# Token operands of an FFN's down projection: split slice by slice in the next unit, in program order with the weights' splits

## The chip, the cores and the metric

The kernel runs on one core of a Trainium2 chip. The metric is the time of one execution on the device in microseconds. The kernel before was timed in three runs: median 2538.07 us (2537.52 to 2538.74). Traces come from one execution each, taken with the hardware profiler. The names of the engines are those of the profile: PE is TensorE, PEld its weight loads, ACT ScalarE, DVE VectorE, POOL GpSimd, and SP (SPq) the engine whose queue issues nearly all transfers.

## The reference

One layer of a streaming encoder over 576 tokens (512 of a new stream and 64 of a running one, the 16 meta tokens apart), in float32:

```python
o_d = rmsnorm(o_d, lp['diff_subln_g']) * (1.0 - lam_init)
mix = jnp.concatenate([o_d.reshape(B, L, D_DIFF), o_m.reshape(B, L, D_MLA)], axis=-1)
x = x + mix @ lp['w_out']
h = rmsnorm(x, lp['norm_ffn_g'])
x = x + (jax.nn.silu(h @ lp['ffn_w_gate']) * (h @ lp['ffn_w_up'])) @ lp['ffn_w_down']
```

Ahead of it stand an input projection and two groups of attention heads, which the change leaves as they are; behind it one more rmsnorm. The model is 2048 wide (16 rows of 128), the hidden layer 5632 (44 rows of 128). The change is in the last line.

## The kernel before

**Products.** A float32 operand is split into a high part in fp32r, which ScalarE writes (an ACTIVATE copy: `wh` of a weight, `bh` of a token operand), and a low part, which VectorE writes (source minus high part: `wl`, `bl`). A product of two such operands is three matmuls: high by high and token-low by weight-high at line 1126, token-high by weight-low at line 1130. Nearly every instruction of the other engines is issued by a recording wrapper, so that its line is 125; the tiles' names tell them apart.

**Gate and up.** The 5632 hidden columns are worked in 22 units `u` of 256. A unit has two turns, gate (g) and up (u). A turn is one call of `winograd`: a 2 x 2 block product by seven products p instead of eight, in the order p = 1, 2, 4, 5, 6, 3, 7 (`ORDER`, `WIDE`). The tokens stand as two halves of 288 columns. For each p, `lhs(p)` makes the weight operand and splits it (`split_weights`): p = 1, 2, 4 from the loaded weights `raw` (two loads of 1 MB a turn), p = 5, 6, 3, 7 from sums `ws` of them, made by GpSimd and VectorE. Then come 16 matmuls with `wh` and 8 with `wl`, and `take(p, banks)` brings the finished accumulator `m` to the tile `c`: by a ScalarE copy for p = 1, 4, 5, 6, by VectorE additions for p = 2, 3, 7. There are two buffers each of `wh` and `wl`. Behind the gate turn `gated` scales c by the tokens' norm `rb2` (VectorE), takes the silu (ScalarE, c to c) and scales again (GpSimd).

**Down operands.** Behind the up turn GpSimd multiplies the two results and forms four differences of their quarters. The product goes to DRAM as `actspill`, the differences as `sumspill`. The down stage loads each quarter or difference again (144 KB), and `builder` splits it there into `bh` and `bl`, for the block of units that comes next.

**Down.** The 22 units go in blocks of 4, 4, 4, 4, 4, 2. A block runs over eight steps d of 256 output columns; in the first five blocks a step is seven products of 12 matmuls (`down_rows`, in the order `CHAIN`), added to the accumulators `y`, which start from `x2spill`. The last block is plain (`plain_rows`, line 205), with the final norm and the output tiles `ot` behind it (`finish`, transposes at line 1394). The operands of the first block are fetched and split during the up turn of unit 21; after it the pools of the gate and up stage are closed and others opened ("the switch").

**What sets the order.** The framework's scheduler orders each engine's instructions by their dependences and a model of their times, except where an instruction is marked:

```python
    def __getattr__(self, name):
        issue = getattr(self.engine, name)

        def call(*args, **kwargs):
            ins = issue(*args, **kwargs)
            return self.tc.keep_in_program_order(ins) if self.ordered else ins
```

A marked instruction stays behind the one that was written just before it on its engine. All matmuls are marked, and, in the down stage, the splits of token operands (`pin`). The weights' splits and the copies of accumulators are not. All engines execute their own list in its order.

Of the kernel before, what the change touches and what calls it, by code (L numbers as in the profile page):

```python
# [2 lines left out]

# [16 lines left out]
P = 128  # L20
# [111 lines left out]
def encoder_step(  # L132
# [196 lines left out]
    sumspill = dp.tile([FC // 2, P, 4, QH], F32, name="sumspill")  # L329
    mspill = dp.tile([KC, P, TQ], F32, name="mspill")  # L330
# [673 lines left out]
    rb2 = rw.tile([P, TQ], F32, name="rb2")  # L1004
    sq2 = rw.tile([P, TQ], F32, name="sq2")
# [13 lines left out]

    def operand(m, p, src):  # L1020
        hi = bc.tile([P, QH], F32R, name=f"bh{p}_{m}")
        lo = bc.tile([P, QH], F32R, name=f"bl{p}_{m}")
        pin(S.activation(hi, src, AF.Copy))
        pin(V.tensor_tensor(lo, src, f32(hi), op=ALU.subtract))
        operands[m, p] = (hi, lo)
# [41 lines left out]

    def winograd(wpool, spool, raws, slots, take, banks=None, engine=V, step=lambda: None, stag=("ws", 3),
                 chain=()):
# [29 lines left out]
        vs = [r.rearrange("p (m t) (f c) -> p t f m c", t=2, f=2) for r in raws]  # L1099
        n = sum(v.shape[3] for v in vs)  # L1100
        a11, a12, a21, a22 = ([v[:, t, f] for v in vs] for f in range(2) for t in range(2))
        sums = {}

        def lhs(p):
            if p in (1, 2, 4):
                return split_weights(n, {1: a11, 2: a12, 4: a22}[p])
            if p == 5:
                s = sums[1] = subtotal(n, G, ALU.add, a21, a22)
            elif p == 6:
                s = sums[2] = subtotal(n, engine, ALU.subtract, [sums[1]], a11)  # L1110
            elif p == 3:
                s = subtotal(n, V, ALU.subtract, a12, [sums[2]])
            else:
                s = subtotal(n, G, ALU.subtract, a11, a21)
            return split_weights(n, [s])

        shared = {}
        for p, name in chain or [(p, p) for p in ORDER]:
            new = name not in shared
            if first:  # L1120
                shared[name] = banks[p] = shared[name] if not new else pmt()[:, 0:QH]
            wh, wl = lhs(p)
            for k in range(n):
                hi, lo = operands[slots[k], p]
                for x in (hi, lo):
                    PE.matmul(banks[p], wh[:, k, :], x, start=first and new and k == 0 and x is hi, stop=False,  # L1126
                              skip_group_check=not new)
            for k in range(n):
                hi, lo = operands[slots[k], p]
                PE.matmul(banks[p], wl[:, k, :], hi, start=False, stop=last and k == n - 1,  # L1130
                          skip_group_check=not new)
            if last:
                take(p, banks)
            step()
# [51 lines left out]
    close_ma()  # L1186
    fb, close_fb = pool("fb", "right")


    def stile():  # L1190
        return fr.tile([P, QH], F32, name="s", tag="s", bufs=4)

    def combined(c11, c12, c21, c22, chain):
# [15 lines left out]
        def take(p, banks):  # L1209
            if p == 1:  # L1210
                s[1] = stile()
                S.activation(s[1], banks[1], AF.Copy)
            elif p == 6:
                s[2] = stile()
# [13 lines left out]
    def builder(m0, count, plain, ahead, by_product=False):  # L1228

        srcs = {}  # L1230
        for m in range(m0, m0 + count):
            quarter = [actspill[2 * m + f, :, c] for f in range(2) for c in (slice(0, QH), slice(QH, TQ))]
            if plain:
                for p, src in zip((1, 2, 4, 5), quarter):
                    srcs[m, p] = src
            else:
                for p, src in zip(ORDER, (quarter[0], quarter[2], sumspill[m, :, 2], sumspill[m, :, 0],
                                          sumspill[m, :, 1], quarter[3], sumspill[m, :, 3])):
                    srcs[m, p] = src
        order = [p for p, _ in CHAIN]  # L1240
        todo = sorted(srcs, key=lambda mp: order.index(mp[1])) if by_product else list(srcs)

        def fetch(n):
            for m, p in todo[n:n + 1]:
                hi = bc.tile([P, QH], F32R, name=f"bh{p}_{m % 8}")
                lo = bc.tile([P, QH], F32R, name=f"bl{p}_{m % 8}")
                load(f32(lo), srcs[m, p])
                operands[m % 8, p] = (hi, lo)

        for n in range(ahead):  # L1250
            fetch(n)
        for n, (m, p) in enumerate(todo):
            fetch(n + ahead)
            hi, lo = operands[m % 8, p]
            pin(S.activation(hi, f32(lo), AF.Copy))
            yield
            pin(V.tensor_tensor(lo, f32(lo), f32(hi), op=ALU.subtract))
            yield
# [17 lines left out]

    turn = 0
    norm = token_norm()
    start = builder(0, blocks[0], False, 4, True)
    for u in range(FC // 2):  # L1280
        out = {}
        for which, wsrc in (("g", w_gate), ("u", w_up)):
# [9 lines left out]
            take = combined(*quarters(c[:, 0, :], c[:, 1, :]), chain)  # L1292
            done = [0]

            def step():
                if u == 0 and which == "u":
                    next(norm, None)
                if u == FC // 2 - 1 and which == "u":
                    done[0] += 1
                    if done[0] > 2:  # L1300
                        for _ in range(2 * blocks[0]):
                            next(start, None)

            if first:
                winograd(fw, fb, raws, range(4, 8), take, banks0, step=step)
            else:
                winograd(fw, fb, raws, range(8), take, step=step, chain=chain)
# [4 lines left out]
        if u == 0:  # L1312
            gated(g)
        for f in range(2):
            G.tensor_tensor(w[:, f, :], w[:, f, :], g[:, f, :], op=ALU.mult)
            if u < FC // 2 - 1:
                store(actspill[2 * u + f], w[:, f, :])
        if u < FC // 2 - blocks[-1]:
# [6 lines left out]
            store(sumspill[u], t)  # L1325
    for _ in start:
        pass
    for f in range(2):
        store(actspill[FC - 2 + f], out["u"][:, f, :])
    close_fb()  # L1330
    close_rw()
    yy, close_yy = pool("yy", "right")
    close_fw()
    yp, close_yp = pool("yp")

    y = []

    def plain_rows(m0, n, d, hs, slots, done):
# [3 lines left out]
        for g in range(0, n, 2):  # L1342
            for f in range(2):
                wh = yp.tile([P, 4, P], F32R, name="wh", tag="wh", bufs=2)
                wl = yp.tile([P, 4, P], F32R, name="wl", tag="wl", bufs=2)
# [6 lines left out]
        for f in range(2):  # L1352
            for h in hs:
                c = y[2 * d + f][:, h * QH:(h + 1) * QH]
# [3 lines left out]
    def down_rows(m0, n, d, slots, step):  # L1358
        raws = [load_raw(fr, w_down, m0 * 256, 2 * n, d * 256, 2)]
        y11, y12, y21, y22 = quarters(y[2 * d], y[2 * d + 1])  # L1360
# [6 lines left out]
        winograd(yp, yp, raws, slots, take, step=step, chain=CHAIN)  # L1367
# [3 lines left out]

    def squares(i, h):
        c = y[i][:, h * QH:(h + 1) * QH]
        if i == 0:
            sqs[h] = stile()
            G.tensor_tensor(sqs[h], c, c, op=ALU.mult)
        else:
            t = stile()
# [4 lines left out]
    def finish(h, ahead):  # L1383
# [6 lines left out]
        def turned(q, j):  # L1390
            o, n = tok[h][j]
            ps = pmt()
            for k in range(4):
                PE.transpose(ps[0:n, k * P:(k + 1) * P], y[q * 4 + k][:, o:o + n], ident)
# [7 lines left out]
        vc = yp.tile([P, 3], F32, name=f"vc{h}")  # L1402
        rc = yp.tile([P, 3], F32, name=f"rc{h}")
# [7 lines left out]
        for i, (q, j) in enumerate(groups):  # L1411
            o, n = tok[h][j]
            ps = held.pop(0) if held else turned(q, j)
            ot = yp.tile([P, 512], F32, name="ot", tag="ot", bufs=OT_BUFS)
# [13 lines left out]
    for bi, n in enumerate(blocks):  # L1428
        slots = [(first + k) % 8 for k in range(n)]
        if bi + 1 < len(blocks):  # L1430
            build = builder(first + n, blocks[bi + 1], bi + 2 == len(blocks), 4)
# [4 lines left out]
            for d in range(KC // 2):  # L1436
                if bi == 0:
                    for i in (2 * d, 2 * d + 1):
                        y.append(yy.tile([P, TQ], F32, name=f"y{i}"))
                        load(y[i], x2spill[i])  # L1440
# [3 lines left out]
        else:  # L1444
            before = iter(())
# [10 lines left out]
    close_yp()  # L1456
    close_fr()
    close_yy()
    close_bc()
# [74 lines left out]
```

## Time and profile before

| | us |
|---|---|
| median of three runs | 2538.07 |
| the profiled execution | 2533.22 |
| its span, first to last instruction | 2531.3 |
| mean granted TensorE clock | 0.992 |
| gate and up stage ends, down begins (the switch) | 1961.7 |
| last block of the down stage begins | about 2447 |

A row of windows gives the stretch, its length, then for each engine the busy time and, in brackets, its instructions; then the granted TensorE clock (1 is full), the share of the DMA engines and GB/s. A row of the timeline gives start, duration, engine, line, operation, out<-in, the shape, a count, and in square brackets the idle time ahead of it with what ended it. A row of the waits gives who waited for what: us in total, times, the longest. A row of groups gives the count, the busy time with the mean of one in ns, and the idle time ahead with what ended it.

The profile's duration of a matmul is modelled and longer than its share of the pipeline: a matmul of 288 columns shows 0.29 us, while they follow each other every 0.133 us.

### The profile page before, as it was taken

What the parts mean: (1) busy time and instruction counts of PE and PEld (TensorE: products, weight loads), DVE (VectorE), ACT (ScalarE), POOL (GpSimd) and SP (SyncE); (2) the same over time, 40 slices, a digit from 0 to 9 for tenths busy, and PEclk for the clock granted to TensorE, in tenths of its full rate; (3) what the DMA queues carried; (4) which work ended last, traced back from release to release, by engine and by line L of the source; (5) the groups of instructions that cost most, each with busy time, mean ns of one, the idle gap of its engine ahead of it and who ended that gap; (6) DMA issues with size and microseconds to landing.
All of it is one profiled execution on the core that took longest, in us unless ns stands there. A gap on an engine that the chain in (4) does not pass through costs nothing. (4 is left out here: it accounts for less than half of the span.)

```text
span 2531.3 us, 44872 instructions
## 1 busy us (share of the span) xinstructions
PE 2440.7 (96%) x17847; PEld 2381.8 (94%) x17847; DVE 1800.2 (71%) x2826; ACT 1106.6 (44%) x2008; POOL 744.3 (29%) x621
## 2 busy tenths in 40 slices
PE   8999999989999999999999999999999899999997
PEld 6999999988999888999999999999999899999997
DVE  5555555556555568877777777777777899999975
ACT  5343333333433444444444444444445444444445
POOL 0000000010000265644545454454543222222236
PEclk9999999999999999999999999999999899999999
DMA  7432232334322553333433333333335642542334
GB/s 216 141 93 80 81 87 83 82 111 120 100 84 76 166 151 112 125 126 121 137 109 117 117 125 132 119 125 100 128 128 167 207 150 84 159 157 84 111 100 150
DMA packets 330116, 307.73 MB, mean 122 GB/s; under 512 B 24708, under 2 KB 298507, under 8 KB 329907
## 3 DMA queue, kind: packets, MB, share of 16 engines
q1 hardware_dynamic: 329346, 302.80, 38.3%
q8 instruction: 140, 2.29, 0.4%
q0 software_dynamic: 560, 2.06, 0.2%
q14 instruction: 70, 0.57, 0.1%
HBM read 250.82 MB, written 56.68 MB: 121 GB/s over the span
## 5 line engine op out<-in xcount | busy, mean ns | idle before, releaser
L1126 PE MATMUL m<-bh,wh 128*128 128x288 f32 x3584 | 968.0, 296 | 11.0 <-DMA bl<-sumspill 8.4
L1126 PE MATMUL m<-bl,wh 128*128 128x288 f32 x3584 | 967.5, 295 | 0.0
L1126 PEld LDWEIGHTS m<-bh,wh 128*128 128x128 f32 x3584 | 673.9, 188 | 11.8 <-ACT wh L125 11.7
L1126 PEld LDWEIGHTS m<-bl,wh 128*128 128x128 f32 x3584 | 677.4, 189 | 0.1
L1130 PE MATMUL m<-bh,wl 128*128 128x288 f32 x3584 | 585.5, 298 | 17.1 <-DVE wl L125 14.5
L1130 PEld LDWEIGHTS m<-bh,wl 128*128 128x128 f32 x3584 | 512.2, 188 | 30.6 <-DVE wl L125 30.1
L1095 POOL TENSOR_TENSOR ws<-raw 128x512 f32<-128x512 f32 x256 | 344.1, 1352 | 599.1 <-DVE wl L125 319.2
L125 ACT ACTIVATE wh<-ws 128x512 fp32r<-128x512 f32 (+1 forms) x340 | 288.8, 849 | 447.6 <-PE m L1126 296.8
L125 DVE TENSOR_TENSOR wl<-ws,wh 128x512 fp32r<-128x512 f32 (+1 forms) x340 | 378.8, 1114 | 114.3 <-ACT wh L125 114.3
L125 DVE TENSOR_TENSOR wl<-raw,wh 128x512 fp32r<-128x512 f32 x416 | 403.7, 984 | 26.1 <-ACT wh L125 16.8
L125 ACT ACTIVATE wh<-raw 128x512 fp32r<-128x512 f32 x416 | 249.7, 626 | 306.2 <-PE m L1126 279.9
L108 PE MATMUL ps<-xh,wh 128*128 128x296 f32 x960 | 221.4, 312 | 1.2 <-ACT wh L125 1.2
L108 PE MATMUL ps<-xh,wl 128*128 128x296 f32 x960 | 210.7, 301 | 1.2 <-DVE wl L125 1.2
L108 PE MATMUL ps<-xl,wh 128*128 128x296 f32 x960 | 210.5, 301 | 0.0
L108 PEld LDWEIGHTS ps<-xh,wh 128*128 128x128 f32 x960 | 157.1, 191 | 5.5 <-ACT wh L125 1.7
L108 PEld LDWEIGHTS ps<-xh,wl 128*128 128x128 f32 x960 | 157.0, 190 | 2.2 <-DVE wl L125 2.2
L125 DVE TENSOR_TENSOR y<-y,m 128x288 f32<-128x288 f32 x312 | 139.6, 447 | 27.2 <-PE m L1130 18.0
L108 PEld LDWEIGHTS ps<-xl,wh 128*128 128x128 f32 x960 | 157.5, 190 | 0.0
L125 DVE TENSOR_TENSOR ws<-ws,raw 128x512 f32<-128x512 f32 x128 | 92.3, 722 | 83.6 <-POOL ws L1095 77.2
L125 DVE TENSOR_TENSOR wl<-wr,wh 128x1024 fp32r<-128x1024 f32 (+1 forms) x110 | 117.7, 1070 | 36.9 <-ACT wh L125 35.4
L125 ACT ACTIVATE wh<-wr 128x1024 fp32r<-128x1024 f32 (+1 forms) x110 | 101.7, 929 | 61.8 <-PE ps L108 52.0
L1273 POOL TENSOR_TENSOR c<-c,rb 128x576 f32<-128x576 f32 x44 | 73.2, 1664 | 164.8 <-ACT c L125 162.3
(359 smaller groups left out, 3342.5 us busy)
## 6 DMA issues: line engine op xcount, KB each, us to landing
raw<-in_ffn_w_gate SPq DMA_DIRECT2D x44, 1024.0 KB, 6.9
raw<-in_ffn_w_up SPq DMA_DIRECT2D x44, 1024.0 KB, 5.9
raw<-in_ffn_w_down SPq DMA_DIRECT2D x40, 1024.0 KB, 5.4
wr<-in_w_in SPq DMA_DIRECT2D x60, 512.0 KB, 4.0
actspill<-c SPq DMA_DIRECT2D x44, 288.0 KB, 2.1
sumspill<-c SPq DMA_DIRECT2D x20, 576.0 KB, 2.8
bl<-sumspill SPq DMA_DIRECT2D x80, 144.0 KB, 3.5
bl<-actspill SPq DMA_DIRECT2D x68, 144.0 KB, 3.9
```

Source lines behind the costliest of these rows:

```text
L108: self.tc.keep_in_program_order(self.pe.matmul(out, lhsT, rhs, start=start, stop=stop))
L125: ins = issue(*args, **kwargs)
L1095: engine.tensor_tensor(w[:, k:k + m, :], pick(xs), pick(ys), op=op)
L1126: PE.matmul(banks[p], wh[:, k, :], x, start=first and new and k == 0 and x is hi, stop=False, skip_group_check=not new)
L1130: PE.matmul(banks[p], wl[:, k, :], hi, start=False, stop=last and k == n - 1, skip_group_check=not new)
L1273: G.tensor_tensor(g[:, f, :], g[:, f, :], rb2, op=ALU.mult)
```

## The change

- The seven token operands of units 2 to 19 are made from the on-chip tiles in the next unit: a generator `parts` yields one piece at a time (a ScalarE copy, a VectorE subtraction, a store of 288 KB to `partspill`), three of them in the gate turn, after p = 6, 3, 7, and four in the up turn, after p = 1, 2, 4, 5. The down stage loads high and low part ready-made (`fetcher`). Units 0 and 1 (`WHOLE`) are still stored whole and split in the last up turn, and units 20 and 21, the plain block, as before.
- From unit 3 on (`in_order[0] = u > WHOLE`) the weights' splits are marked, as are the pieces.
- The first accumulators y0 to y4 and the first two loads of `w_down` are issued before the switch; y5 to y15 in one go behind the first step.
- The pools of `wh`, `wl` and `ws` stay open through the switch; a split of four rows takes half a tile of eight, so that the down stage has four buffers of each.
- In `finish` each `ot` has a tile of its own.

```diff
         def split_weights(n, srcs):
-            wh = wpool.tile([P, n, P], F32R, name="wh", tag="wh", bufs=2)
-            wl = wpool.tile([P, n, P], F32R, name="wl", tag="wl", bufs=2)
+            wh, wl = weight_tiles(wpool, n)
+            S.ordered = V.ordered = in_order[0]
             k = 0
             for s in srcs:
                 split(wh[:, k:k + s.shape[1], :], wl[:, k:k + s.shape[1], :], s)
                 k += s.shape[1]
+            S.ordered = V.ordered = False
             return wh, wl
...
+    def parts(u, srcs):
+
+        for p in ORDER:
+            b = fb.tile([P, 2, QH], F32R, name="parts", tag="parts", bufs=2)
+            S.ordered = V.ordered = True
+            S.activation(b[:, 0, :], srcs[PIECE[p]], AF.Copy)
+            V.tensor_tensor(b[:, 1, :], srcs[PIECE[p]], f32(b[:, 0, :]), op=ALU.subtract)
+            S.ordered = V.ordered = False
+            store(partspill[u, :, PIECE[p]], f32(b))
+            yield
...
+            in_order[0] = u > WHOLE
+            if ending:
+                Q.ordered = True
+                fetch_raw(0, blocks[0], 0)
...
             def step():
                 if u == 0 and which == "u":
                     next(norm, None)
-                if u == FC // 2 - 1 and which == "u":
-                    done[0] += 1
-                    if done[0] > 2:
-                        for _ in range(2 * blocks[0]):
-                            next(start, None)
+                done[0] += 1
+                if which == "u" or done[0] > 4:
+                    next(pieces, None)
+                if ending:
+                    next(start)
...
-            store(sumspill[u], t)
+            if u < WHOLE:
+                store(sumspill[u], t)
+            else:
+                pieces = parts(u, [b11, b12, b21, b22] + [t[:, i, :] for i in range(4)])
...
+                if bi == 0 and d == 1:
+                    Q.ordered = False
+                    close_fb()
+                    yy, close_yy = pool("yy", "right")
+                    y[5] = [y234[:, 3 * TQ:3 * TQ + QH], yy.tile([P, QH], F32, name="y5")]
+                    for half, src in zip(y[5], halves(x2spill[5])):
+                        load(half, src)
+                    for i in range(6, KC):
+                        accumulator(i, yy.tile([P, TQ], F32, name=f"y{i}"))
```

In the lists that follow, each engine's instructions stand in their order: out<-in with buffer numbers, the shape, and in brackets what kinds of semaphores an instruction waits for (PE: TensorE's, DVE: VectorE's, DMAHW: a transfer's).

ScalarE in a gate turn, before, from the split of p = 2 to the copy of p = 5 (`wh<-raw` splits p = 2 and 4, `wh<-ws` p = 5, 6 and 3; `c<-m` are the copies, of p = 1, 4 and 5):

```order
L125 ACTIVATE wh_15822<-raw_15784 128x512 [waits DVE_49,PE_49]
L125 ACTIVATE wh_15822<-raw_15786 128x512
L125 ACTIVATE wh_15854<-raw_15784 128x512 [waits DVE_49,PE_49]
L125 ACTIVATE wh_15854<-raw_15786 128x512
L125 ACTIVATE c_15788<-m_15789 128x288 [waits DMAHW5_49,PE_49]
L125 ACTIVATE wh_15889<-ws_15886 128x1024 [waits DVE_49,PE_49,Pool_49]
L125 ACTIVATE wh_15921<-ws_15918 128x1024 [waits DVE_49,PE_49]
L125 ACTIVATE c_15788<-m_15853 128x288 [waits PE_49]
L125 ACTIVATE wh_15953<-ws_15950 128x1024 [waits DVE_49,PE_49]
L125 ACTIVATE c_15788<-m_15885 128x288 [waits PE_49]
```

The same place after, from the copy of p = 1 to that of p = 6:

```order
L125 ACTIVATE c_15391<-m_15392 128x288 [waits PE_49]
L125 ACTIVATE wh_15425<-raw_15387 128x512 [waits DVE_49]
L125 ACTIVATE wh_15425<-raw_15389 128x512
L125 ACTIVATE wh_15457<-raw_15387 128x512 [waits DVE_49]
L125 ACTIVATE wh_15457<-raw_15389 128x512
L125 ACTIVATE c_15391<-m_15456 128x288 [waits PE_49]
L125 ACTIVATE wh_15492<-ws_15489 128x1024 [waits DVE_49,Pool_49]
L125 ACTIVATE c_15391<-m_15488 128x288 [waits PE_49]
L125 ACTIVATE wh_15524<-ws_15521 128x1024 [waits DVE_49]
L125 ACTIVATE c_15391<-m_15392 128x288 [waits PE_49]
```

Before, the splits of p = 2 and 4 stood ahead of the copy of p = 1, and those of p = 5 and 6 ahead of the copy of p = 4. Now the copy of p = 1 stands ahead of the split of p = 2, and the copies of p = 4 and 5 directly ahead of the splits of p = 5 and 6.

ScalarE between a gate turn and its up turn, before (the rows behind the copy `c_15788<-m_15789` of p = 6 are the next turn's splits from `raw_16021` and `raw_16023`, and the two silus `c_15788<-c_15788`):

```order
L125 ACTIVATE wh_15953<-ws_15950 128x1024 [waits DVE_49,PE_49]
L125 ACTIVATE c_15788<-m_15885 128x288 [waits PE_49]
L125 ACTIVATE wh_15985<-ws_15982 128x1024 [waits DVE_49,PE_49,Pool_49]
L125 ACTIVATE c_15788<-m_15789 128x288 [waits PE_49]
L125 ACTIVATE wh_16027<-raw_16021 128x512 [waits DMAHW1_49,DVE_49,PE_49]
L125 ACTIVATE wh_16027<-raw_16023 128x512 [waits DMAHW5_49]
L125 ACTIVATE c_15788<-c_15788 128x576 [waits DVE_49]
L125 ACTIVATE wh_16059<-raw_16021 128x512 [waits PE_49,Activation_49]
```

And after, where `parts` are pieces, the silus are the row with x2, and the up turn's first split is that from `raw_15636`:

```order
L125 ACTIVATE wh_15560<-ws_15557 128x1024 [waits DVE_49]
L125 ACTIVATE parts_15589<-c_15138 128x288 [waits DMAHW1_49,Pool_49]
L125 ACTIVATE wh_15596<-ws_15593 128x1024 [waits DVE_49,Pool_49]
L125 ACTIVATE parts_15626<-c_14889 128x288 [waits DMAHW5_49,DVE_49]
L125 ACTIVATE c_15391<-c_15391 128x576 [waits DVE_49] x2
L125 ACTIVATE wh_15642<-raw_15636 128x512 [waits DMAHW2_49,PE_49,Activation_49]
L125 ACTIVATE wh_15642<-raw_15638 128x512 [waits DMAHW3_49]
```

Both silus have moved ahead of the up turn's first split; before, that split stood ahead of both, and that of p = 2 ahead of the second.

SP's queue at the switch, before, from the second load of `w_down` on:

```order
L125 DMA raw<-in_ffn_w_down 128x8x256
L125 DMA bl_0_21607<-sumspill 128x288
L125 DMA bl_1_21612<-sumspill 128x288
L125 DMA bl_2_21617<-sumspill 128x288
L125 DMA bl_3_21622<-sumspill 128x288
L125 DMA actspill<-c 128x576 x2
L125 DMA bl_4_21676<-sumspill 128x288
L125 DMA bl_5_21900<-sumspill 128x288
L125 DMA bl_5_22033<-actspill 128x288
L125 DMA bl_6_22165<-actspill 128x288
L125 DMA y_21645<-x2spill 128x576
L125 DMA y_21647<-x2spill 128x576
```

After, the same place:

```order
L125 DMA raw<-in_ffn_w_down 128x8x256
L125 DMA y_21971<-x2spill 128x576 x3
L125 DMA actspill<-c 128x576 x2
L125 DMA b_4_21995<-partspill 128x576
L125 DMA b_4_22015<-partspill 128x576
L125 DMA b_4_22052<-partspill 128x576
L125 DMA b_4_22073<-partspill 128x576
L125 DMA b_4_22109<-partspill 128x576
L125 DMA y_21971<-x2spill 128x288
L125 DMA y_22115<-x2spill 128x288
```

which goes on with eight more accumulators, and then:

```order
L125 DMA y_22134<-x2spill 128x576
L125 DMA y_22136<-x2spill 128x576
L125 DMA b_4_22154<-partspill 128x576
L125 DMA b_4_22193<-partspill 128x576
L125 DMA b_5_22268<-partspill 128x576
L125 DMA raw<-in_ffn_w_down 128x8x256
```

The third load of `w_down` stands behind all accumulators of the stage; before, it stood behind ten of the sixteen, and the transfers of operands were half the size.

More of the change, by code (lines that the diff above doesn't have):

```diff
@@ L1003, in encoder_step @@
     rw, close_rw = pool("rw", "right")
-    rb2 = rw.tile([P, TQ], F32, name="rb2")
-    sq2 = rw.tile([P, TQ], F32, name="sq2")
+    sq2 = rw.tile([P, TQ], F32, name="sq2", tag="rows", bufs=2)
+    rb2 = rw.tile([P, TQ], F32, name="rb2", tag="rows", bufs=2)
     operands = {}
@@ L1066, in pmt, with weight_tiles @@
         return pm.tile([P, 512], F32, name="m", tag="m")
+    spare = []
+    in_order = [False]
+    def weight_tiles(wpool, n):
+        if n == 8 or not spare:
+            both = [wpool.tile([P, 8, P], F32R, name=x, tag=x, bufs=2) for x in ("wh", "wl")]
+            if n == 8:
+                return both
+            spare.append([w[:, 4:8, :] for w in both])
+            return [w[:, 0:4, :] for w in both]
+        return spare.pop()
     def winograd(wpool, spool, raws, slots, take, banks=None, engine=V, step=lambda: None, stag=("ws", 3),
@@ new lines, in fetch_whole, with act_quarter, starter, whole @@
+    def fetch_whole(m, p, src):
+        operand_tile(m % 8, p)
+        load(f32(operands[m % 8, p][1]), src)
+    def act_quarter(m, q):
+        return actspill[2 * m + q // 2, :, q % 2 * QH:(q % 2 + 1) * QH]
+    def starter():
+        def whole(m, p):
+            q = PIECE[p]
+            return act_quarter(m, q) if q < 4 else sumspill[m, :, q - 4]
+        todo = [p for p, _ in CHAIN]
+        for i in range(len(todo) + 2):
+            if i < len(todo):
+                for m in range(blocks[0]):
+                    if m < WHOLE:
+                        fetch_whole(m, todo[i], whole(m, todo[i]))
+                    else:
+                        fetch_parts(m, todo[i])
+            if i > 1:
+                for m in range(WHOLE):
+                    split_in_place(m, todo[i - 2])
+            yield
@@ L1256, in builder @@
+    def builder(m0, count, ahead):
+        todo = [(m, p, act_quarter(m, q)) for m in range(m0, m0 + count) for q, p in enumerate((1, 2, 4, 5))]
+        for n in range(ahead):
+            fetch_whole(*todo[n])
+        for n, (m, p, _) in enumerate(todo):
+            if n + ahead < len(todo):
+                fetch_whole(*todo[n + ahead])
             yield
-            pin(V.tensor_tensor(lo, f32(lo), f32(hi), op=ALU.subtract))
+            split_in_place(m % 8, p)
             yield
@@ L1275, in encoder_step, with fetch_raw, accumulator @@
     blocks = [4, 4, 4, 4, 4, 2]
+    WHOLE = 2
+    def parts(u, srcs):
+        for p in ORDER:
+            b = fb.tile([P, 2, QH], F32R, name="parts", tag="parts", bufs=2)
[4 more added lines that the diff above has]
+            store(partspill[u, :, PIECE[p]], f32(b))
+            yield
+    fetched = {}
+    def fetch_raw(m0, n, d):
+        fetched[m0, d] = load_raw(fr, w_down, m0 * 256, 2 * n, d * 256, 2)
+    y = {}
+    def accumulator(i, tile):
+        y[i] = halves(tile)
+        load(tile, x2spill[i])
     turn = 0
     norm = token_norm()
-    start = builder(0, blocks[0], False, 4, True)
+    start = starter()
+    pieces = iter(())
     for u in range(FC // 2):
@@ L1292, in encoder_step, with take @@
             take = combined(*quarters(c[:, 0, :], c[:, 1, :]), chain)
+            ending = u == FC // 2 - 1 and which == "u"
+            in_order[0] = u > WHOLE
+            if ending:
+                Q.ordered = True
+                fetch_raw(0, blocks[0], 0)
+                accumulator(0, rw.tile([P, TQ], F32, name="y0", tag="rows", bufs=2))
+                combine, w, g = take, quarters(c[:, 0, :], c[:, 1, :]), out["g"]
+                g = quarters(g[:, 0, :], g[:, 1, :])
+                def take(p, banks):
+                    combine(p, banks)
+                    if p in (2, 7, 3, 4):
+                        q = {2: 0, 3: 1, 4: 2, 7: 3}[p]
+                        G.tensor_tensor(w[q], w[q], g[q], op=ALU.mult)
             done = [0]
@@ L1401, in finish @@
         pc = pmt()
[L1402 to L1403 removed]
+        vc = room(others)[:, 0:3]
+        rc = room(others)[:, 0:3]
         V.memset(vc, 1.0)
@@ L1436, in encoder_step @@
             for d in range(KC // 2):
[L1437 to L1440, printed above, removed]
+                if bi == 0 and d == 1:
[7 more added lines that the diff above has]
+                        accumulator(i, yy.tile([P, TQ], F32, name=f"y{i}"))
+                if (first, d) not in fetched:
+                    fetch_raw(first, n, d)
                 down_rows(first, n, d, slots, step)
@@ L1444, in encoder_step @@
         else:
+            rest = [m for m in range(8) if m not in slots]
+            sums = itertools.cycle([f"b{p}_{rest[-1]}" for p in ORDER])
+            others = iter([f"b{p}_{m}" for m in rest[-2::-1] for p in ORDER])
             before = iter(())
```

110 lines of the change are left out of this document (58 added, 52 removed).

## The prediction

> **What bounds the kernel now.** I read the page's first part, then windows of the stage that the change reworks, then TensorE's waits. TensorE is busy for 96% of the span; the windows say where it isn't.
>
> ```profile
> PE 2440.7 (96%) x17847; PEld 2381.8 (94%) x17847; DVE 1800.2 (71%) x2826; ACT 1106.6 (44%) x2008; POOL 744.3 (29%) x621
> ```
> ```profile
> core 0: us, PE busy (x) PEld busy (x) DVE busy (x) ACT busy (x) POOL busy (x), PEclk, DMA share, GB/s
> 1150.00:1961.00 811.00, 811.00 (x6097) 811.00 (x6097) 610.22 (x708) 361.87 (x564) 393.27 (x283) 1.00 0.38 125
> 1950.00:2000.00 50.00, 40.51 (x280) 39.69 (x279) 41.79 (x78) 24.48 (x51) 10.77 (x8) 0.86 0.85 279
> 2000.00:2050.00 50.00, 48.67 (x358) 47.45 (x358) 47.01 (x85) 23.92 (x45) 10.86 (x8) 1.00 0.30 94
> 2400.00:2450.00 50.00, 49.87 (x375) 49.55 (x374) 41.21 (x69) 19.07 (x31) 9.31 (x8) 1.00 0.29 87
> ```
> ```profile
> PE m L1130 <- DVE wl L125: 12.1, 25, 0.9
> PE m L1126 <- DMA bl<-sumspill: 8.4, 1, 8.4
> PE m L205 <- DVE wl L125: 3.0, 8, 0.7
> PE m L1394 <- ACT ot L125: 2.5, 1, 2.5
> PE m L205 <- ACT wh L125: 1.9, 3, 1.4
> ```
>
> From 1150 to 1961 (gate and up) TensorE loses nothing: 811 of 811 us at 6097 matmuls, 0.133 us each. A product there is 24 matmuls, 3.19 us, the first 16 on the high weight part. Behind 1961 (down) it loses at the switch, then by the many short waits for VectorE's low parts, then in the last block. So the change can win only behind 1961, and whatever it makes late ahead of 1961 comes on top in full.
>
> **Ahead of 1961, the splits.** How far ahead the splits run today:
>
> ```profile
> L125 ACT ACTIVATE wh<-raw 128x512 fp32r<-128x512 f32 x416 | 249.7, 626 | 306.2 <-PE m L1126 279.9
> ```
> ```profile
> 1919.47 1.16 ACT L125 ACTIVATE wh<-raw 128x512 fp32r<-128x512 f32 x2 [2.04 <-PE m L1126]
> 1920.54 0.41 ACT L125 ACTIVATE c<-m 128x288 f32<-128x288 f32 x1
> 1922.71 1.06 ACT L125 ACTIVATE wh<-ws 128x1024 fp32r<-128x1024 f32 x1 [1.76 <-PE m L1126]
> ```
> ```profile
> 1919.27 1.24 PE L1130 MATMUL m<-bh,wl 128*128 128x288 f32 x8
> 1920.34 0.29 PE L1126 MATMUL m<-bh,wh 128*128 128x288 f32 x1
> ```
>
> ScalarE sits idle until TensorE gives a weight buffer back, so a split is ready about a product early. The split at 1919.47 is for the product that begins near 1923.5. The accumulator copy (c<-m) of the product that ends at 1920.34 comes 0.20 us behind that end, and no split that TensorE needs soon stands behind it.
>
> After the change, from unit 3 on, a split keeps its place behind whatever was written before it on its engine. In the order of ScalarE the copy of p1 stands ahead of the split of p2, that of p4 ahead of p5's, that of p5 ahead of p6's, that of p6 ahead of p3's. Each copy waits for the last matmul of its own product. So TensorE ends the product, stands, and cannot start the next until ScalarE has copied and split. The buffers are still two; the lead is gone. The prices:
>
> ```profile
> L125 ACT ACTIVATE wh<-ws 128x1024 fp32r<-128x1024 f32 x145 | 153.9, 1061 | 248.9 <-PE m L1126 167.5 <-DVE ws L125 31.7 <-DVE wl L125 29.1
> L125 DVE TENSOR_TENSOR c<-c,rb 128x576 f32<-128x576 f32 x36 | 28.1, 780 | 0.0
> L125 ACT ACTIVATE c<-c 128x576 f32<-128x576 f32 x36 | 24.4, 679 | 35.9 <-DVE c L125 35.9
> L125 DVE TENSOR_TENSOR bl<-bl,bh 128x288 fp32r<-128x288 f32 x22 | 9.9, 502 | 0.2 <-ACT bh L125 0.2
> ```
> ```profile
> 1944.25 0.39 ACT L125 ACTIVATE c<-m 128x288 f32<-128x288 f32 x1
> 1944.54 1.44 ACT L125 ACTIVATE bh<-bl 128x288 fp32r<-128x288 f32 x4
> ...
> 1969.77 0.63 ACT L125 ACTIVATE wh<-raw 128x512 fp32r<-128x512 f32 x1 [1.08 <-DMA actspill<-c]
> ```
> ```profile
> 1970.45 0.61 PE L1126 MATMUL m<-bh,wh 128*128 128x288 f32 x1 [8.43 <-DMA bl<-sumspill]
> ```
> ```profile
> 1917.35 0.82 DVE L125 TENSOR_TENSOR c<-c,m 128x288 f32<-128x288 f32 x2 [0.23 <-PE m L1130]
> ```
>
> The copy begins 0.20 behind the end and holds ScalarE 0.29 (1944.25 to 1944.54). The first half of a split from raw takes 0.63, a split of a sum 1.06. TensorE follows 0.05 later (1969.77 + 0.63 to 1970.45). A new operand piece, the same shape as bh<-bl, adds 1.44/4 = 0.36 where it stands between copy and split.
> - p1 to p2: 0.20 + 0.29 + 0.63 + 0.05 = 1.17, in the up turn with a piece 1.53.
> - p4 to p5, p5 to p6, p6 to p3: 0.20 + 0.29 + 1.06 + 0.05 = 1.60; with a piece 1.96 (p6 to p3 of the gate turn; the first two in the up turn).
> - p2 to p4, p3 to p7: no copy between, and VectorE's low parts are wanted only 16 matmuls (2.1 us) on: 0.
> - Gate turn to up turn: the two silus (c<-c) stand ahead of the up turn's first split, behind VectorE's two additions of p7 (0.20 + 0.82), a piece (0.50) and the scaling c<-c,rb (0.78); then silu 0.68, split 0.63, 0.05. That is 3.66 by full lengths; successors start up to 0.1 early, as at 1944.54, so I take 3.4.
>
> Gate turn 1.17 + 1.60 + 1.60 + 1.96 + 3.4 = 9.7; up turn 1.53 + 1.96 + 1.96 + 1.60 = 7.05. A unit loses 16.8 of 44.6 us. Units 3 to 20 have pieces: 18 x 16.8 = 302. Unit 21 has no pieces, and two copies ahead of splits of sums in its up turn: 1.17 + 3 x 1.60 + 3.0 + 2 x 1.60 = 12. **Together +314.** Had the pieces alone been added and the splits kept their lead, this would be 0: 7 x 0.36 us of ScalarE and 7 x 0.50 of VectorE per unit fit beside TensorE (VectorE 610 of 811 busy).
>
> **What gaps do to the matmuls behind them.**
>
> ```profile
> 2163.45 0.80 PE L1130 MATMUL m<-bh,wl 128*128 128x288 f32 x4 [0.49 <-DVE wl L125]
> 2164.09 0.29 PE L1126 MATMUL m<-bh,wh 128*128 128x288 f32 x1
> ```
> ```profile
> 400.92:404.34 3.42, 1.69 (x18) 1.36 (x17) 3.38 (x10) 2.61 (x6) 0.00 (x0) 1.00 0.26 69
> 404.34:407.75 3.41, 3.41 (x15) 3.41 (x15) 2.64 (x7) 1.24 (x3) 0.15 (x1) 0.50 0.57 163
> 974.36:977.78 3.42, 1.75 (x12) 1.33 (x10) 3.23 (x5) 1.63 (x4) 3.03 (x4) 1.00 1.06 383
> 977.78:981.19 3.41, 3.25 (x23) 3.08 (x24) 3.23 (x6) 1.71 (x4) 0.84 (x2) 1.00 0.14 45
> ```
>
> After a gap four matmuls take 0.64 instead of 0.53: 0.11 per gap, 9 gaps a unit, 19 units: **+19**. And the granted clock falls: a stretch with TensorE busy 1.69 of 3.4 us was followed by one at 0.50, a stretch with 1.75 was not. A gap of 3.4 us leaves such a stretch nearly each time; one of 1.6 leaves at least 1.8; one of 1.96 is at the edge. A stretch at half clock takes 15 matmuls where 26 fit, a loss of 1.5 us; at 1970.45 it lasted two. I take 2 us at each of the 19 gate-to-up gaps, **+38**. Lower end 0; upper end 19 x 4 gaps of 1.9 or more x 3 us = 228, if the edge falls the other way. [...]
>
> **Behind 1961.**
>
> ```profile
> 1960.78 1.23 PE L1130 MATMUL m<-bh,wl 128*128 128x288 f32 x8
> ...
> 1977.63 0.41 PE L1126 MATMUL m<-bh,wh 128*128 128x288 f32 x1
> ```
> ```profile
> 1992.00:1996.00 4.00, 4.00 (x32) 4.00 (x32) 3.91 (x7) 2.32 (x5) 1.29 (x1) 1.00 1.06 388
> ```
> ```profile
> L125 DVE TENSOR_TENSOR bl<-bl,bh 128x288 fp32r<-128x288 f32 x113 | 75.4, 667 | 0.0
> ```
>
> - Switch: 8.4 us of waiting for stored sums, then half clock until 1977.63. The window 1950 to 2000 has 280 matmuls, of 377 at full pace: 97 x 0.133 = 12.9 lost, nearly all here. Units 2 and 3 now come split, 0 and 1 are split in the last up turn, the first rows of y are there: this goes. But w_down's third raw now stands on SP's queue behind 24 transfers of 288 KB and one more raw: 9.2 MB at 0.388 MB/us (1992 to 1996) is 24 us from the switch, and the third step is due about 19 behind it (two steps of 84 matmuls, less the lead of its splits). New stall some 6, and clock 2.5: net −4. Bounds −13 and 0.
> - Middle, 1996 to 2380: VectorE drops 75 us of bl splits in the middle alone. 2000 to 2050 has 358 matmuls, 2400 to 2450, where the operands are few, 375: 17 x 0.133 = 2.3 per 50 us, x 7.7 = 18; the windows that run poorer bring it to about 24. I take **−24**.
> - Last block and tail: deeper weight buffers against 3.0 + 1.9 of waiting, one tile for each ot against 2.5: −6; bounds −7 and 0. In all **−34**.
>
> **Sum.** +314 + 19 + 38 − 34 = +337 on the profiled execution's 2533.2 us gives 2870; the median of the runs is 2538.1, 4.9 more: **2875 us**.
>
> **Rivals.**
> - The lead survives: the order binds nothing, since a copy is released before the split behind it is needed, and the pieces hide under TensorE. Then only −34 is left: 2504. It decides where a gap averages under 34/171 = 0.2 us (171 = 9 x 19). For it speaks ScalarE's low load (44%). Against it: the copy starts 0.20 behind the product's end (1920.54), and TensorE has no other product to run. [...] Chance 6 in 100.
> - The clock stays down through most gaps of 1.9: 228 in place of 38, about 3065. Speaks for it: 1.69 and 1.75 lie close. Against: two of the wider gaps are never in one stretch. 14 in 100.
> - The gaps are there at half the size, because a split's first half or an earlier release hides more than I see: 314 becomes 157, about 2700. 6 in 100.
> - The change does nothing, gaps of 0.2 balance the 34: 2538. 2 in 100.
>
> **The numbers.** My forecast has 72 in 100, at 2785 (no clock, no slow matmuls, gaps a tenth shorter: −38 − 19 − 31) to 2950. The range runs on to 3010 for part of the clock case. Faster by over 0.2% (about what a measurement of this kernel can tell from no change): 0.06, within 0.02, slower 0.92.
>
> **What would show it.** In the profile after: gate and up windows at some 70% TensorE, with waits of m for wh (ScalarE) 130 to 170 times 1.1 to 2 us, and 19 of 3 to 4; the copy c<-m directly ahead of wh in ScalarE's timeline; stretches at clock 0.5 behind the gate turns; a down stage with few waits for wl. Wrong would be a gate and up stage at full TensorE, or waits there that name VectorE or a transfer.

## The result and the profile after

The changed kernel takes 3021.98 us in the median of four runs (3018.14 to 3023.86) against 2537.8 us before: 1.191 times as long, with an interval of 1.189 to 1.193. The profiled execution took 3021.6 us, span 3019.8, mean granted clock 0.940. The direction was the one forecast, and the main mechanism (TensorE waiting for ScalarE's splits behind the copies) is there; the time is 147 us over the forecast and 12 over its range, and two of the terms that make it up, the low parts and the clock, were wrong.

The page's first part and, from its second, the granted clock in 40 slices:

```profile
PE 2606.8 (86%) x17847; PEld 2504.9 (83%) x17847; DVE 1740.5 (58%) x2826; ACT 1070.9 (35%) x2008; POOL 730.0 (24%) x623
...
PEclk9999999999999998888888888888888899999999
```

Three windows (in gate and up over 1250 us, one stretch of 50 us in it, and one in the down stage), then TensorE's waits from 1050 us to the end:

```profile
1200.00:2450.00 1250.00, 938.40 (x5841) 889.03 (x5842) 590.24 (x780) 366.33 (x644) 366.04 (x276) 0.88 0.26 89
2000.00:2050.00 50.00, 37.04 (x237) 35.16 (x236) 27.67 (x38) 15.80 (x28) 13.92 (x10) 0.90 0.28 98
2550.00:2600.00 50.00, 50.00 (x378) 49.82 (x376) 40.34 (x72) 18.50 (x32) 13.26 (x9) 1.00 0.78 259
```
```profile
PE m L1146 <- ACT wh L125: 305.0, 170, 4.5
PE m L1150 <- DVE wl L125: 32.7, 37, 1.0
PE m L1146 <- DVE y L125: 3.9, 2, 2.9
PE m L1503 <- DVE b L125: 2.8, 2, 1.6
PE m L1491 <- ACT b L125: 2.7, 1, 2.7
PE m L205 <- DVE wl L125: 2.6, 6, 0.4
```

Before, the gate and up stage had no wait of TensorE and 377 matmuls in 50 us; in the stretch shown it now has 237. The 170 waits for ScalarE's high parts had been forecast as 130 to 170. Of the 37 waits for VectorE's low parts 36 lie in gate and up (31.9 us up to the switch); waits there that name VectorE were what the prediction had called a sign of being wrong. In the down stage the waits for `wl` fall from 12.1 to 0.8 us, and TensorE is full in its middle.

Where the forecast saw the copy ahead of the split, the timeline has it, and TensorE between them (ScalarE from the copies of p = 5 and 6 in unit 10's gate turn; TensorE in the same stretch):

```profile
1636.85 0.41 ACT L125 ACTIVATE c<-m 128x288 f32<-128x288 f32 x1 [3.55 <-PE m L1150]
1637.16 1.05 ACT L125 ACTIVATE wh<-ws 128x1024 fp32r<-128x1024 f32 x1
1641.75 0.41 ACT L125 ACTIVATE c<-m 128x288 f32<-128x288 f32 x1 [3.55 <-PE m L1150]
1642.06 0.43 ACT L125 ACTIVATE parts<-c 128x288 fp32r<-128x288 f32 x1
1642.39 1.05 ACT L125 ACTIVATE wh<-ws 128x1024 fp32r<-128x1024 f32 x1
```
```profile
1638.26 2.38 PE L1146 MATMUL m<-b,wh 128*128 128x288 f32 x16 [1.45 <-ACT wh L125]
1640.48 1.23 PE L1150 MATMUL m<-b,wl 128*128 128x288 f32 x8
1643.49 2.39 PE L1146 MATMUL m<-b,wh 128*128 128x288 f32 x16 [1.77 <-ACT wh L125]
1645.72 1.24 PE L1150 MATMUL m<-b,wl 128*128 128x288 f32 x8
...
1654.36 4.21 PE L1146 MATMUL m<-b,wh 128*128 128x288 f32 x16 [4.03 <-ACT wh L125]
```

From 1638.26 to 1643.49 one product takes 5.23 us instead of 3.19. At full clock 16 matmuls behind a wait are 2.38 long in this view (at 1638.26); the 4.21 at 1654.36, behind the wait for the silus, are at half clock (a granted clock of 0.50 from 1652.04 to 1658.87). The rows start in the order of ScalarE's list, and by the tiles' names so do, in the whole trace, all 1858 ACTIVATE instructions of ScalarE, 2245 TENSOR_TENSOR of VectorE, 556 of GpSimd and 921 transfers issued by SP, each in that of its engine's list.

Since both kernels run the same 17847 matmuls in the same order, the time of each can be set against that of its twin. At the end of the last up turn the changed kernel is 507.8 us late, of which 2.7 stood before unit 3 began: **gate and up cost 505**. At the last matmul it is 488.5 late: **the down stage gained 19**.

### The profile page after: what moved, and what is told of

Same layout as the page of the kernel before. It is cut to its first block, busy times and chain, and to the rows that moved or that the text cites. A ratio compares the mean times of both kernels' runs of the same rounds, so it can differ in the third digit from the quotient of the medians.

```text
span 3019.8 us, 44775 instructions
## 1 busy us (share of the span) xinstructions
PE 2606.8 (86%) x17847; PEld 2504.9 (83%) x17847; DVE 1740.5 (58%) x2826; ACT 1070.9 (35%) x2008; POOL 730.0 (24%) x623
## 5 line engine op out<-in xcount | busy, mean ns | idle before, releaser
L1146 PE MATMUL m<-b,wh 128*128 128x288 f32 x7168 | 1154.2, 314 | 312.1 <-ACT wh L125 307.6
L1146 PEld LDWEIGHTS m<-b,wh 128*128 128x128 f32 x7168 | 1062.2, 203 | 356.5 <-ACT wh L125 349.9
L1150 PE MATMUL m<-b,wl 128*128 128x288 f32 x3584 | 619.8, 310 | 35.0 <-DVE wl L125 34.9
L1150 PEld LDWEIGHTS m<-b,wl 128*128 128x128 f32 x3584 | 549.1, 202 | 48.0 <-DVE wl L125 48.0
L125 DVE TENSOR_TENSOR wl<-ws,wh 128x512 fp32r<-128x512 f32 (+1 forms) x340 | 345.2, 1026 | 267.9 <-ACT wh L125 267.5
L125 DVE TENSOR_TENSOR wl<-raw,wh 128x512 fp32r<-128x512 f32 x416 | 333.8, 832 | 82.5 <-ACT wh L125 80.5
L125 ACT ACTIVATE c<-m 128x288 f32<-128x288 f32 x172 | 70.4, 410 | 782.0 <-PE m L1150 781.9
L125 DVE TENSOR_TENSOR parts<-c,parts 128x288 fp32r<-128x288 f32 x126 | 66.1, 525 | 223.8 <-ACT parts L125 223.8
L125 DVE TENSOR_TENSOR c<-c,m 128x288 f32<-128x288 f32 x172 | 74.0, 450 | 165.7 <-PE m L1150 164.9
L125 DVE TENSOR_TENSOR ws<-ws,raw 128x512 f32<-128x512 f32 x128 | 107.9, 868 | 26.8 <-POOL ws L1115 22.9
```

## The experiments

Two theories: **A**, the place of the weights' splits behind the copies (and additions) of the product before stops TensorE, and the clock falls with it; **B**, the pieces' own work and stores (126 of 288 KB) load the engines and the queues. Of e2 to e5 each was timed once; the others are medians of four to six runs.

**e1: the weights' splits unmarked.**

```diff
-            in_order[0] = u > WHOLE
+            in_order[0] = False
```

> The changed kernel, but the weights' splits are not marked (the pieces still are). If the marked weight splits cost the time (theory A), gate and up come back to full TensorE and only the gain behind the switch is left: 2500 to 2530 us, half clock nearly none. If the pieces' own work or their stores cost it (theory B), it stays above 2950 us.

2515.44 us, ratio 0.992 (0.990 to 0.993). Gate and up are full again, with all pieces in place:

```profile
1150.00:1961.00 811.00, 811.00 (x6098) 811.00 (x6097) 671.65 (x816) 398.67 (x673) 425.19 (x288) 1.00 0.43 145
```

VectorE's busy time there rose from 610 to 672 us and cost TensorE nothing. B falls. What the change was worth without the mark stands here: 0.8% faster. What e1 still loses:

```profile
PE m L1146 <- ACT wh L125: 6.4, 1, 6.4
```

**e2 and e3: only one engine's half marked.**

```diff
-            S.ordered = V.ordered = in_order[0]
+            S.ordered = in_order[0]        # e2
+            V.ordered = in_order[0]        # e3
```

> The changed kernel with only ScalarE's half of each weight split (the high part) marked, VectorE's low part free. Theory A (the accumulator copy ahead of the split on ScalarE is the main wait, with a clock loss behind it): 2930 to 2990 us, waits of m for wh about 300 us, waits for wl a few. If VectorE's order were the main one: near 2530 us.

> The changed kernel with only VectorE's half of each weight split (the low part) marked, ScalarE's high part free. Theory A: low parts wait behind the additions of p7 and p2, some 1 to 2 us a unit, and nothing on wh: 2520 to 2590 us. If the two waits only come together: near 2510 us. If VectorE's order is the main one: above 2900 us.

e2: 2928.7 us, 93 less than with both marked and 1 under the expected range. Its waits for high parts stay, those for low parts (32.7 us) go; half-clock time (at a granted clock of 0.50) falls from 317 to 198 us (between 1050 us and the end of the up turns, counted from the clock's record, here and below). e3: 2660.4 us, a miss: 70 above the expected range. Waits of e2 and e3, from 1050 us to the end:

```profile
PE m L1146 <- ACT wh L125: 294.0, 171, 6.7
PE m L1150 <- DVE wl L125: 0.8, 1, 0.8
```
```profile
PE m L1150 <- DVE wl L125: 81.0, 58, 3.0
```

VectorE's order alone makes 81 us of waits and 89 us of half clock, in all 145 us against e1. With both marked the waits for low parts are 32.7 us and not 81; that TensorE comes later to them, when part of them is ready, is argued. So the two don't add up (at the end of the up turns e2 is 412 us behind e1, e3 143, both together 505).

**e4: the kernel before with nothing but the mark.**

```diff
+            S.ordered = V.ordered = in_order[0]
             for s in srcs:
...
+            S.ordered = V.ordered = False
             return wh, wl
...
+            in_order[0] = u > 2
```

> The kernel before with nothing but the mark: weight splits of units 3 to 21 in program order, no pieces, no other pools, loads as before. Theory A: gaps without a piece in them 1.17 + 3 x 1.6 + 3.0 in the gate turn and 1.17 + 3 x 1.6 in the up turn, 15 us x 19 = 284, some 35 for low parts, 20 slow first matmuls, 60 to 120 of clock: 2920 to 3000 us. Theory B: 2538 us.

2960.2 us. Waits up to the switch:

```profile
PE m L1130 <- ACT wh L125: 267.1, 169, 3.5
PE m L1134 <- DVE wl L125: 31.9, 36, 1.0
```

The mark alone, without one piece, costs the kernel before some 424 us (2960.2 against 2536.4 on the same chip). With 267 + 169 x 0.26 = 311 the gaps are a little over the 284 + 20 expected (the 0.26 is read below). Of the 80 us up to the full change in gate and up, 33 are longer waits (300.6 instead of 267.1), from the pieces that stand between copy and split; they weigh only because something waits behind them. The other 47 fit the longer half clock, 317 us instead of 191: by e5 below, 314 us of it cost 113, so 126 cost some 45 (an estimate).

**e5: the gaps filled.** Idle matmuls of 224 columns at the places where TensorE waits; they write beside the accumulators in their banks. This kernel does not compute the layer's output; it is there for its time alone.

```diff
+            fill = {2: 8, 5: 10, 6: 10, 3: 10, 1: 26 * (in_order[0] == "u")}.get(p, 0) if in_order[0] in ("g", "u") else 0
...
+                x = operands[slots[0], p][0]
+                for _ in range(count):
+                    PE.matmul(full[name][:, QH:512], x[:, 0:P], x[:, 0:512 - QH], start=True, stop=True,
+                              skip_group_check=True)
...
+            keep_busy(fill)
             wh, wl = lhs(p)
...
+            keep_busy(8 * (in_order[0] == "g" and p == 1))
...
-            in_order[0] = u > WHOLE
+            in_order[0] = which if u > WHOLE and not (u == FC // 2 - 1 and which == 'u') else u > WHOLE
```

> The changed kernel with idle matmuls (224 columns, their result is never read) in TensorE's list where it waits for a split in units 3 to 21: 8 to 10 at each of the copies, 26 at the silus, 8 ahead of p1's low parts in gate turns. The waits for the splits stay as long as they are. If the half clock comes from low use of TensorE in a stretch (theory A): half-clock time falls from 310 us to under 40, no slow first matmuls, 2880 to 2920 us. If the clock falls for another reason, or the gaps only look like waits: 3020 us or more.

2909.0 us, 113 less than the changed kernel, with some 2,000 matmuls more. The window and two products:

```profile
1200.00:2300.00 1100.00, 1000.77 (x7477) 968.03 (x7477) 576.29 (x759) 352.38 (x621) 353.40 (x266) 1.00 0.29 98
```
```profile
1623.59 2.38 PE L1157 MATMUL m<-b,wh 128*128 128x288 f32 x16 [0.67 <-ACT wh L125]
1625.80 1.24 PE L1162 MATMUL m<-b,wl 128*128 128x288 f32 x8
1626.88 1.27 PE L1149 MATMUL m<-b 128*128 128x224 f32 x10
1628.82 2.38 PE L1157 MATMUL m<-b,wh 128*128 128x288 f32 x16 [0.67 <-ACT wh L125]
```

The clock is 1.00 (half clock falls from 317 to 3 us), and from product to product it is still 5.23 us (1623.59 to 1628.82), the same as without the fillers: the gaps are the order's, and 113 us are the clock's. The first matmuls behind a gap stay slow (2.38 for 16, against 2.28 at 1618.45, where no gap is ahead), which I had expected to go.

**e6: the marks kept, the split one product ahead.** The next product's split is written ahead of the copy of the one before, across turns too. The core of the edit:

```diff
             wh, wl = lhs(p)
+            pend()
...
-            if last:
-                take(p, banks)
-            step()
+            def pend(p=p):
+                if last:
+                    take(p, banks)
+                step()
```

> The changed kernel with all its marks kept, but the split of the next product is written (and so ordered) ahead of the accumulator's copy or addition of the product before it, across the turns too. Theory A (it is the place of the copy in the order, not the mark as such): the gaps at the copies go; the two silus still stand ahead of the second split of the up turn, about 0.5 us a unit: 2510 to 2545 us, little half clock. If the mark itself costs, because it takes freedom from the scheduler elsewhere: above 2700 us.

2558.5 us, ratio 1.009 (1.007 to 1.012): 464 us back with every mark in place, though 13 above the range. Waits up to the switch, and ScalarE between a gate and an up turn:

```profile
PE m L1148 <- ACT wh L125: 33.4, 20, 2.8
```
```profile
1507.45 0.45 ACT L125 ACTIVATE parts<-c 128x288 fp32r<-128x288 f32 x1 [1.36 <-DMA partspill<-parts]
1509.42 0.69 ACT L125 ACTIVATE c<-c 128x576 f32<-128x576 f32 x1 [1.52 <-DVE c L125]
1512.64 0.68 ACT L125 ACTIVATE c<-c 128x576 f32<-128x576 f32 x1 [2.54 <-DVE c L125]
1513.23 1.13 ACT L125 ACTIVATE wh<-raw 128x512 fp32r<-128x512 f32 x2
```

One wait a unit is left, that for the second silu: 1.5 us, where I had written 0.5.

**e7: e1 with the accumulators' loads spread over the steps.**

```diff
-                    for i in range(6, KC):
-                        accumulator(i, yy.tile([P, TQ], F32, name=f"y{i}"))
                 if (first, d) not in fetched:
                     fetch_raw(first, n, d)
+                if bi == 0 and d:
+                    for i in range(6 if d == 1 else 2 * d + 4, min(2 * d + 6, KC)):
+                        accumulator(i, yy.tile([P, TQ], F32, name=f"y{i}"))
```

> The kernel with free weight splits (e1) and the accumulators y6 to y15 loaded two at each step behind that step's raw weights, so that the third load of w_down has 8 transfers of 288 KB fewer ahead of it on SP's queue. If the 6.4 us wait at the third step is that queue (theory A): 2.36 MB at 0.38 MB/us = 6 us less plus the half clock behind it, 2504 to 2510 us. If the load waits for its buffer: 2515 us, as e1.

2510.4 us, ratio 0.992 (0.989 to 0.994), the same ratio as e1's on another chip: the times don't tell the two apart, the traces do. From the switch to the matmul that ran at 2050 before, e7 gains 10.2 us on its twins and e1 2.3, and the wait of 6.4 us is gone (1965 to 2040):

```profile
PE m L1146 <- ACT wh L125: 0.3, 1, 0.3
```

**e8, e9, e10: on one chip.** e8 is e6 with the silus behind the up turn's second split as well and the accumulators spread; e9 is e1 and e10 is e7, again. The edit of e8 against e6, without the accumulators' part:

```diff
+                for f in later[:]:
+                    later.remove(f)
+                    f()
                 if last:
                     take(p, banks)
...
-                    gated(c)
+                    later.append(lambda: gated(c))
```

> e6 (marks kept, splits one product ahead) with the gate turn's scaling and silus also behind the second split of the up turn, and the accumulators spread as in e7. Theory A: the one wait a unit that e6 kept (1.5 us, with its slow first matmul 1.75) goes, 19 x 1.75 = 33, the load's 6.4 and the half clock behind it some 9: 2558 - 42 = 2516, range 2506 to 2525. If the marks had a cost of their own: above 2540 us.

> The kernel of e1 once more, to stand on one chip beside e8 and e10: 2515 us, a ratio of 0.990 to 0.993.

> The kernel of e7 once more beside e9. If the accumulators' queue cost what the trace of e1 shows (6.4 us and a half clock of 10 us behind it, some 9 us together), it is 6 to 10 us under e9; if the difference of the two earlier traces was chance, within 2 us of it.

e8: 2524.3 us, ratio 0.996 (0.994 to 0.997), at the upper end of what was expected; waits for high parts 8.1 us in 17 places. So a kernel with all marks can beat the kernel before, if the order is written with a lead; it stays 17 us over e10, which has the same loads and no marks on the weights' splits. e9: 2515.9 us, 0.992 (0.991 to 0.994). e10: 2507.6 us, 0.991 (0.988 to 0.993), 8 us under e9 as expected, but its runs go from 2504.6 to 2529.8, so the intervals overlap and this is shown by the traces rather than by the times: the wait is 0.3 us in e10 and 4.4 in e9, and from the switch to the 2050 of before e10 gains 9.5 us, e9 2.2. e10 is the fastest version found: 0.9% under the kernel before.

## Why the prediction came out as it did

**What bounds.** Right: all the loss stands in gate and up, which had nothing to give, and e1 shows that the pieces hide there.

**+314 for the gaps of ScalarE's order.** Nearly right. TensorE waited 300.6 us, 169 times, up to the switch. A wait of 1.45 stands for a product of 4.90 (1638.26 less 1633.36) instead of 3.19, so each wait counts 0.26 more than the view says, the slow first matmul (0.11) among it: 300.6 + 169 x 0.26 = 345, against 314 + 19. The 1.71 us lost at that product are what was forecast (1.60 + 0.11); the 12 us over come mostly from the gap behind the gate turn, a wait of 4.03 where 3.4 had been taken.

**0 for the low parts.** This is a step that failed: "VectorE's low parts are wanted only 16 matmuls (2.1 us) on: 0". It was argued for p2 to p4 and p3 to p7, and the up-to-gate turn wasn't looked at on VectorE. There the split of p1 stands behind a subtraction for the sums and the two additions of p7, beside GpSimd's products (VectorE, then GpSimd, then TensorE, unit 10):

```profile
1616.41 1.29 DVE L125 TENSOR_TENSOR ws<-raw,ws 128x512 f32<-128x512 f32 x1
1617.63 0.81 DVE L125 TENSOR_TENSOR c<-c,m 128x288 f32<-128x288 f32 x2
1618.36 2.50 DVE L125 TENSOR_TENSOR wl<-raw,wh 128x512 fp32r<-128x512 f32 x2
```
```profile
1618.51 1.80 POOL L1408 TENSOR_TENSOR c<-c 128x576 f32<-128x576 f32 x1 [1.36 <-DVE c L125]
```
```profile
1619.09 0.80 PE L1150 MATMUL m<-b,wl 128*128 128x288 f32 x4 [0.76 <-DVE wl L125]
1620.91 1.02 PE L1150 MATMUL m<-b,wl 128*128 128x288 f32 x4 [1.02 <-DVE wl L125]
```

These are 1.8 us a unit of plain waiting, 32 in all and 41 with 0.26 each, and a half-clock stretch stands behind them. e2 prices VectorE's mark, both together, at 93 us.

**+38 for the clock.** The term that was mis-sized most: 113 by e5. I gave one gap a unit 2 us; the rival with half clock at most of the wider gaps had 228, and the measured 113 lie between. A unit has three places (the low-part wait, the gap behind the gate turn, one gap in the up turn), and 17 us of half clock (the clock's record: 6.83, 6.83 and 3.41 us in each of units 5 to 20). Stretches of the length of a half-clock stretch, unit 10: the three ahead of a fall, each with the one behind it, and two with no fall behind them (1634.98 and 1641.80):

```profile
1617.91:1621.32 3.41, 1.63 (x11) 1.16 (x10) 2.95 (x4) 0.00 (x0) 2.73 (x2) 1.00 0.00 0
1621.32:1624.74 3.42, 2.40 (x10) 2.05 (x10) 1.29 (x2) 2.48 (x5) 1.70 (x3) 0.50 0.00 0
...
1634.98:1638.39 3.41, 1.97 (x15) 1.73 (x14) 0.15 (x1) 1.35 (x2) 2.18 (x2) 1.00 0.36 100
...
1641.80:1645.22 3.42, 1.73 (x13) 1.73 (x14) 2.12 (x3) 2.92 (x5) 0.51 (x1) 1.00 0.78 281
1645.22:1648.63 3.41, 3.41 (x27) 3.41 (x27) 2.50 (x5) 0.44 (x1) 0.00 (x0) 1.00 0.00 0
1648.63:1652.04 3.41, 1.71 (x12) 1.31 (x10) 3.41 (x7) 0.69 (x1) 1.62 (x1) 1.00 0.23 87
1652.04:1655.46 3.42, 1.10 (x4) 1.10 (x5) 2.15 (x3) 1.72 (x3) 1.46 (x2) 0.50 0.23 86
...
1672.52:1675.94 3.42, 1.64 (x13) 1.41 (x12) 1.58 (x2) 1.69 (x3) 0.91 (x1) 1.00 0.73 235
1675.94:1679.35 3.41, 3.41 (x16) 3.41 (x15) 0.10 (x1) 0.00 (x0) 2.55 (x2) 0.50 1.07 374
```

Stretches with TensorE busy for 1.63, 1.71 and 1.64 us had a fall behind them, those with 1.97 and 1.73 none. So a gap of 1.6 did no harm here, as forecast; of the three gaps of 1.96 in a unit, "at the edge", the second of the up turn fell on the wrong side (1.64) and that of the gate turn didn't (1.73); and the low-part wait made the third place. Even without that place the 38 was too small: e2 has 198 us of half clock left, some 71 us at e5's price (an estimate). No limit in busy time divides all stretches: 1.71 and 1.73 lie side by side, and the trace of before has one of 2.19 with a fall behind it, beside the 1.69 and 1.75 from which the edge was read:

```profile
851.48:854.90 3.42, 2.19 (x15) 2.04 (x16) 2.83 (x5) 3.16 (x8) 0.00 (x0) 1.00 0.86 254
854.90:858.31 3.41, 3.41 (x16) 3.41 (x15) 1.70 (x3) 0.83 (x2) 0.00 (x0) 0.50 0.91 286
```

Of the 66 half-clock stretches in the changed kernel's trace 27 last 3.41 us and 37 twice that (the clock's record); in the 3.41 us ahead of the four falls in these rows TensorE was busy for 1.63 to 2.19 us.

**Sum of gate and up.** 345 + 41 + 113 = 499 of the 505 measured; forecast 371. So of the 151 us by which the profiled execution passed the forecast (3021.6 against 2870), 75 are the clock's, 41 the low parts', 12 the gaps', 15 the down stage's (below), and 8 are left open.

**−34 behind the switch.** −19 measured. The switch with its new stall was forecast at −4; the lateness goes from 507.8 to 506.1 (at the matmul that ran at 2050 before): −2. The wait for w_down's third load was 4.5 us here and 6.4 in e1, as argued (6), and e7 and e10 confirm the queue. Middle: to 485.0, −21 against −24. Last block and tail: +3.5 against −6. The waits at L205 fell only from 4.9 to 3.8; the wait for `ot`, which I put down to its four buffers, stays at 2.7 (2.5 before) with a tile for each (L1491 <- ACT b), so it wasn't the buffers; and the sums of squares' matmuls wait 2.8 us for VectorE (L1503), where before it was 0.4. Why VectorE is later there was not tried.

## What to carry to other kernels

Keeping an engine in program order fixes not only what comes first but what everything stands behind (424 us in e4): before marking a split, write it ahead of whatever waits for the running product, one product early (e6 2558.5 us, e8 2524.3, against 3022), or leave it to the scheduler (e1, 2515.4). A list of each engine's order, read for instructions that wait for the engine they feed, priced the gaps well here (333 for 345 us). Where a change makes many small gaps, price the clock by the worst stretch at every place of the period (here three places a unit, 17 us at half clock), and look at every engine at every turn's end: the low parts' waits, and the half clock behind them, came from one place that was checked on ScalarE alone.

## What the runs showed of the hardware

**A unit of the changed kernel takes 21 times 3.413 us**, the length of the shortest half-clock stretch in the clock's record. Units 5 to 20 each take 71.63 to 71.75 us, and the three half-clock stretches lie at the same place in all of them, some 5.3, 36 and 60 us from the unit's start. Ten units (716.8 us) behind the first rows above:

```profile
2334.71:2338.12 3.41, 1.63 (x10) 1.17 (x10) 2.91 (x4) 0.00 (x0) 2.76 (x2) 1.00 0.00 0
2338.12:2341.54 3.42, 2.40 (x11) 2.05 (x10) 1.29 (x2) 2.48 (x5) 1.67 (x3) 0.50 0.02 5
```

So a gap near the edge wasn't met by chance here, some of the time, as I had reckoned, but in a fixed pattern. In two more runs the pattern spans several units: those of e2 take mostly 65.1 and 68.0 us in turn (together 39 times 3.413), those of e4 repeat every four (269.7 us, 79 times). What ties the period to the 3.413 us no run tested.

**Idle matmuls made the kernel faster**, 3022 to 2909 us: with them the granted clock is 1.00 from 1200 to 2300 us (e5).

**VectorE beside GpSimd.** Two low parts of 128x512 take 2.50 us beside GpSimd's products (1618.36) and 1.29 at the end of them (1622.93; the last ends at 1623.02):

```profile
1622.93 1.29 DVE L125 TENSOR_TENSOR wl<-raw,wh 128x512 fp32r<-128x512 f32 x2 [2.07 <-ACT wh L125]
```

No run here separated GpSimd's work from other causes of the longer time.
